# Sixteen gate tiles merged into eight pairs of seven block products, in a hybrid Hyena / attention layer on one Trainium2 core

## The chip, the core and the metric

The kernel runs on one core of one Trainium2 chip. TensorE (PE in the profile; its weight loads are PEld) multiplies a stationary 128x128 block, loaded from SBUF, with a moving operand of up to 512 columns and accumulates in PSUM, which has 8 banks of 512 fp32 columns for each of 128 partitions. VectorE (DVE), ScalarE (ACT) and GpSimd (POOL) work beside it, and SyncE (SP) issues most DMAs, in the order of its queue. [...] The metric is the device time of one execution in microseconds (us), less is better.

## The reference

One layer with two branches on the same modulated input, for a prompt of 128 tokens and a latent grid of 512 tokens (8 rows of 64), model width 1024, all in fp32:

```python
def layer_forward(x, cond, ctx_kv, p):
    shift, scale, gate = modulation(cond, p["w_ada"], p["b_ada"])     # silu(cond) @ w_ada + b_ada, in three parts
    h = x * (1 + scale) + shift
    (v_h, x1, x0, g_h), (q, k, v, g_a), m = split_projection(h, p["w_in"], p["conv_w"], p["conv_b"])
    h_fwd, h_bwd = hyena_filters(x.shape[1], ...)
    y_h = hyena_long_conv(v_h, x1, x0, h_fwd, h_bwd, p["hyena_d"])
    y_a = ...      # prompt: softmax attention; latent: window of 8 x 16 with a bias, and all cached context keys
    out = merge_branches(y_h, g_h, y_a.reshape(g_a.shape), g_a, m, p["w_bh"], p["w_ba"], p["w_out"])
    x_new = layer_norm(ALPHA * x + gate * out, p["ln_g"], p["ln_b"])

def merge_branches(y_h, g_h, y_a, g_a, m, w_bh, w_ba, w_out):
    p_h = (y_h * jax.nn.silu(g_h)) @ w_bh
    p_a = (y_a * jax.nn.silu(g_a)) @ w_ba
    m_h, m_a = jnp.split(jax.nn.sigmoid(m), 2, axis=-1)
    return (m_h * p_h + m_a * p_a) @ w_out
```

`split_projection` is one product of h (640 tokens x 1024) with `w_in` (1024 x 10240). Its last 2048 columns are m, the logits of the sigmoid gates m_h and m_a: they are what the change concerns most. `gate`, the third part of the modulation, scales the output of the layer, with one row for the prompt and one for the latent tokens. There are 16 heads of 64.

## The kernel before

**Numbers.** Values are held in fp32. A product is made of three passes in the type fp32r: each operand is split into a high part (ScalarE copy, L98) and a low part (VectorE subtraction, L99), and high x high, high x low and low x high are accumulated. `split` (L97) does it for a weight tile (128x1024: 8 blocks of 128x128 in input depth, k), once per tile.

**Projections.** `proj` (L171) computes 128 output channels for all 640 tokens: `wraw` loads the raw weight tile (512 KB) through SP's queue into a ring of two buffers, `wtile` splits it into rings of two (`wh`) and three (`wl`), and `accumulate` (L161) runs 8 k x 3 passes x 2 halves of 320 tokens, 48 matmuls 128x320 (L166), into the two banks of a double tile of the pool `ps_mm`, of which there are two. Four single banks (`ps_ax`, `aux`) serve attention and the rest. The tiles are numbered in `wall`: T_Q, T_K, T_V, T_GA (attention gates), T_MH and T_MA (the logits of m_h and m_a, 8 tiles each), T_BH and T_BA (the two branch projections), T_WO (the output).

**Stages.** A prologue makes the modulation and h (tiles `hH`, `hL`). Then come four quarters of the Hyena branch, whose results are the 8 rows-of-channels `yh`, kept in SBUF. Attention runs over eight pairs of heads, `attend(j)`, j = 0 to 7; each is cut into steps (`tiled`: scores, softmax on VectorE, ScalarE and GpSimd, and the values of earlier blocks; `turned`: transposes of the probabilities), and `weave` puts main work between the steps: the query, key, value and gate tiles of later heads for j < 7 (`mains`), and for j = 7 the eight T_MH tiles (`mix_h`). The results `ya` (`gated`, L868) stay in SBUF too. After attention come two T_MA tiles (`mix_a`), the eight T_BH tiles (with the merge by m_h at L993, and beside each a step of `gate_rows`), the rest of T_MA alternating with the T_BA tiles (L1022 to L1025), and the output tiles (`out_tile`, 48 matmuls of 512 columns for 128 tokens) with their norms (`norm_tile`).

**The output gate.** `gate_rows` (L970) loads the third part of `w_ada` in eight pieces of 512 KB and multiplies each by the conditioning `st` with 8 fp32 matmuls (`ada`, L231), which the trace holds as 16 records; `gate_bias` (L1002) then spreads the row of each group over 128 partitions with 12 matmuls and adds the bias, into `gbc`.

**What sets the order.** The Tile framework schedules all engines from a model of their times. TensorE's order is the program's own in the prologue and in attention (`manual_schedule`); elsewhere the scheduler orders it too. Loads are pinned to program order on SP while `pinned[0]` is true: until the filters, and not after.

## Time and profile before

| | us |
|---|---|
| median of 3 runs (least to most) | 925.89 (925.84 to 927.05) |
| the profiled execution, of which the span | 925.7, 923.9 |
| prologue, Hyena quarters (to about 390) | 390 |
| attention with its main work (390 to about 670) | 280 |
| rest of T_MH, first T_MA, first T_BH (670 to 704) | 34 |
| T_BH tiles (704 to 759) | 55 |
| T_MA and T_BA tiles, gate bias (759 to 860) | 101 |
| output tiles (860 to 915), last norm and store (to 924) | 64 |

Rows of the profile read like this. A chain row `751.34 7.23 PE mm L166 x48` is a start, a length, and what ran: 48 matmuls of line 166. A group row gives the line, engine, operation, `out<-in` by the program's names, the shape, the count, then the busy time and the mean ns of one, then the idle time ahead of it with what ended it. A wait row `PE pt L824 <- ACT ptsp L914: 0.4, 2, 0.2` is the total, the number and the longest of TensorE's waits for that releaser. A DMA row gives the KB of one and the median time from issue to landing.

### The profile page before, as it was taken

What the parts mean: (1) busy time and instruction counts of PE and PEld (TensorE: products, weight loads), DVE (VectorE), ACT (ScalarE), POOL (GpSimd) and SP (SyncE); (2) the same over time, 40 slices, a digit from 0 to 9 for tenths busy, and PEclk for the clock granted to TensorE, in tenths of its full rate; (3) what the DMA queues carried; (4) which work ended last, traced back from release to release, by engine and by line L of the source; (5) the groups of instructions that cost most, each with busy time, mean ns of one, the idle gap of its engine ahead of it and who ended that gap; (6) DMA issues with size and microseconds to landing.
All of it is one profiled execution on the core that took longest, in us unless ns stands there. A gap on an engine that the chain in (4) does not pass through costs nothing.

```text
span 923.9 us, 16758 instructions
## 1 busy us (share of the span) xinstructions
PE 910.2 (99%) x6856; PEld 877.4 (95%) x6856; DVE 486.4 (53%) x948; ACT 380.4 (41%) x776; POOL 146.2 (16%) x188
## 2 busy tenths in 40 slices
PE   8999999999999999999999999999999999999996
PEld 7899999999999999999999999999999999999885
DVE  4776775693796676445352533432261223335676
ACT  4485455554545334255454544444261112223200
POOL 0011010110010000474454543331000000000000
PEclk9999999999999999999999999999999999999998
DMA  8966664655465113242222221212123343224631
GB/s 320 380 161 135 128 149 98 137 133 123 100 141 126 50 49 85 86 122 67 71 68 69 67 70 58 72 49 70 48 69 113 120 146 99 72 69 116 205 114 69
DMA packets 36553, 102.13 MB, mean 111 GB/s; under 512 B 4316, under 2 KB 13020, under 8 KB 36477
## 3 DMA queue, kind: packets, MB, share of 16 engines
q1 hardware_dynamic: 32300, 86.35, 28.9%
q0 software_dynamic: 4032, 14.68, 9.8%
q8 instruction: 54, 0.88, 0.4%
q14 instruction: 23, 0.18, 0.1%
q10 hardware_dynamic: 144, 0.03, 0.0%
HBM read 97.38 MB, written 3.67 MB: 109 GB/s over the span
## 4 chain that ended last, share of the span: by engine, by line
PE 95%; DVE 2%; ACT 2%; issue 1%; POOL 0%; POOLq 0%
PE mm L166 65%; PE out L1065 6%; PE v L721 5%; PE s L788 2%; PE s L831 2%; PE pt L824 2%; PE ve L732 1%; PE adaT L236 1%; PE adaT L253 1%; PE yb L151 1%; PE yb L153 1%; PE yb L152 1%; PE gate L236 0%; PE fl L384 0%; PE fl L385 0%
## 5 line engine op out<-in xcount | busy, mean ns | idle before, releaser
L166 PE MATMUL mm<-hH,wh 128*128 128x320 f32 x1120 | 263.3, 313 | 0.9 <-ACT hH L312 0.6
L166 PE MATMUL mm<-hH,wl 128*128 128x320 f32 x1120 | 259.7, 310 | 0.4 <-DVE wl L99 0.4
L166 PE MATMUL mm<-hL,wh 128*128 128x320 f32 x1120 | 259.1, 310 | 0.0
L99 DVE TENSOR_TENSOR wl<-raw,wh 128x1024 fp32r<-128x1024 f32 x66 | 81.6, 1237 | 231.9 <-ACT wh L98 231.7
L166 PEld LDWEIGHTS mm<-hH,wh 128*128 128x128 f32 x1120 | 186.7, 188 | 6.2 <-issue 4.2
L166 PEld LDWEIGHTS mm<-hH,wl 128*128 128x128 f32 x1120 | 188.0, 188 | 1.4 <-DVE wl L99 1.1
L166 PEld LDWEIGHTS mm<-hL,wh 128*128 128x128 f32 x1120 | 188.2, 188 | 1.1 <-DVE hL L313 0.5
L98 ACT ACTIVATE wh<-raw 128x1024 fp32r<-128x1024 f32 x66 | 69.8, 1059 | 216.8 <-PE mm L166 95.9
L143 POOL DMA_DIRECT2D wl<-wall x28 | 24.3, 869 | 264.0 <-ACT wl L142 208.8
L144 ACT ACTIVATE wh<-raw 128x1024 fp32r<-128x1024 f32 x28 | 29.7, 1060 | 42.9 <-PE mm L166 42.7
L808 POOL TENSOR_SCALAR p<-p,sm 128x384 f32<-128x384 f32 x32 | 42.1, 1326 | 27.7 <-DVE sm L807 27.7
L1095 POOL TENSOR_TENSOR r<-r,bc 128x64 f32<-128x64 f32 x1 | 0.3, 320 | 249.7 <-ACT r L1094 249.7
L808 POOL TENSOR_SCALAR edge<-edge,sm 128x320 f32<-128x320 f32 x32 | 35.5, 1121 | 0.0
L474 DVE SCALAR_TENSOR_TENSOR x<-zs,pack,x 128x641 f32<-128x641 f32 x32 | 28.3, 884 | 12.1 <-ACT x L472 12.0
L826 ACT ACTIVATE pts<-pt 128x384 f32<-128x384 f32 x64 | 26.2, 502 | 11.0 <-PE pt L824 11.0
L142 ACT ACTIVATE wl<-raw 128x1024 fp32r<-128x1024 f32 x28 | 30.0, 1071 | 0.0
L166 PE MATMUL mm<-yhH,wh 128*128 128x320 f32 x128 | 29.9, 315 | 0.0
L166 PE MATMUL mm<-yaH,wh 128*128 128x320 f32 x128 | 29.2, 309 | 0.0
L166 PE MATMUL mm<-yhL,wh 128*128 128x320 f32 x128 | 29.2, 309 | 0.0
L166 PE MATMUL mm<-yaH,wl 128*128 128x320 f32 x128 | 29.2, 309 | 0.0
L166 PE MATMUL mm<-yaL,wh 128*128 128x320 f32 x128 | 29.2, 309 | 0.0
L166 PE MATMUL mm<-yhH,wl 128*128 128x320 f32 x128 | 29.2, 309 | 0.0
(330 smaller groups left out, 1677.7 us busy)
## 6 DMA issues: line engine op xcount, KB each, us to landing
raw<-wall SPq DMA_DIRECT2D x96, 512.0 KB, 3.6
wl<-wall POOLq DMA_DIRECT2D x28, 512.0 KB, 5.8
ada<-wada SPq DMA_DIRECT2D x16, 512.0 KB, 8.1
gate<-wada SPq DMA_DIRECT2D x8, 512.0 KB, 3.7
wo<-wall SPq DMA_DIRECT2D x8, 512.0 KB, 3.7
xt<-xT SPq DMA_DIRECT2D x8, 320.0 KB, 8.1
dec<-decay SPq DMA_DIRECT2D x20, 128.0 KB, 3.5
x<-xB SPq DMA_DIRECT2D x5, 512.0 KB, 3.8
```

What stands on the lines that cost most here:

```text
L98: hi = nc.scalar.activation(dst_h, src, AF.Copy)
L99: return hi, (eng or nc.vector).tensor_tensor(dst_l, src, f(dst_h), op=ALU.subtract)
L142: nc.scalar.activation(wl, raw[:], AF.Copy, scale=-1.0)
L143: nc.gpsimd.dma_start(wl, a["wall"][i], accum_op=ALU.add)
L144: nc.scalar.activation(wh, raw[:], AF.Copy)
L166: nc.tensor.matmul(ps[hf][:, :HALF], wt[k], x[:, hf * HALF : (hf + 1) * HALF], start=(i == 0 and k == 0), stop=(i == lead[2] and k == NK - ...
L474: nc.vector.scalar_tensor_tensor(d, zs[:, c : c + NG], convw[:, i, c : c + 1], d, op0=ALU.mult, op1=ALU.add)
L721: nc.tensor.matmul(ps[:, t // 2, t % 2 * 256 : t % 2 * 256 + 256], x[:, k, P * t : P * t + P], wk, start=first and t % 2 == 0, stop=last, ...
L788: nc.tensor.matmul(dst[h], x[rows(h), qs], y[rows(h), ks], start=i == 0, stop=i == 2, skip_group_check=True)
L808: nc.gpsimd.tensor_scalar_mul(pv, pv, sm[:, 2:3])
L826: nc.scalar.activation(ptS[:], pt[:, :384], AF.Copy)
L1065: ins = nc.tensor.matmul(dst, m[k][:, c0 : c0 + P], w[:, c : c + n], start=(first and k == 0), stop=(last and k == NK - 1), skip_group_che ...
```

## The change

The line numbers here are those of the changed kernel.

*Pairs.* `mix_h` and `mix_a` are gone. `pair_tile` computes two gate tiles (256 channels) at once. The weights (1024 x 256) and the tokens (1024 x 640) are seen as 2 x 2 blocks: two halves of the depth by two tiles, and two halves of the depth by two halves of the tokens. Seven products of blocks, each 4 k x 3 passes = 12 matmuls 128x320, stand in for eight; the price is sums: of weight blocks (`wsum`, VectorE), of token blocks (`token_sums`, once, beside attention heads 0 and 1), and of results (`u`, `c`). Each product accumulates in one bank. The tanh goes to `c` or `th`, which ScalarE's queue stores to DRAM (`mh_d`, `ma_d`), to be loaded again when the gates are merged.

*Places.* All eight pairs stand in attention: one ahead of the main work of each of j = 2 to 6, three in j = 7. `ps_mm` is four single banks.

*Room.* `yh` is stored to DRAM as it is made and loaded and split again late in attention and after it; `ya` is stored in blocks (`gated`, by SP, for j = 7 by ScalarE) and loaded in the T_BH loop.

*Output gate.* `gate_rows` no longer uses TensorE: at each T_BH tile it loads 128 rows of `w_ada` and does two multiply-adds on VectorE into `gbc`, a partial sum in each partition; the matmuls of `gate_bias`, 12 as before, add up the partitions.

*The end.* From the end of attention `pinned[0]` is true again, so all loads keep program order on SP. The output weights are loaded and split within the T_BA loop and behind it, and used in the order 0, 1, 2, 3, 4, 6, 7, 5.

```diff
-    ps_mm = ctx.enter_context(tc.tile_pool(name="ps_mm", bufs=2, space=PSUM))
+    ps_mm = ctx.enter_context(tc.tile_pool(name="ps_mm", bufs=4, space=PSUM))
...
+    def acc(name):
+        return ps_mm.tile([P, 512], F32, tag="mm", name=name)
...
     def gate_tile(i, dst, eng=None):
-        ps = (yield from proj(i, eng=eng))[2]
-        nc.scalar.activation(two(dst), ps[:, :, :HALF], AF.Tanh, scale=0.5)
-        nc.vector.scalar_tensor_tensor(two(dst), two(dst), 1.0, ps[:, :, :HALF], op0=ALU.add, op1=ALU.mult)
+        ps = yield from proj(i, eng=eng)
+        for p, cs in zip(ps, CS):
+            nc.scalar.activation(dst[:, cs], p[:, :HALF], AF.Tanh, scale=0.5)
+            gate(dst[:, cs], p)
...
             gapped_product(out["yh"][n], out[f"u{n // 2}"][n % 2])
+            nc.sync.dma_start(yh_d[n], out["yh"][n][:])
...
+    def gated(j, o_, *spans):
+        yo = tp.tile([P, P], F32, tag="yo", bufs=3, name=f"yo{j}")
...
+            nc.vector.tensor_tensor(yo[:, c0 : c0 + n], out[f"sg{j}"][:, cols], o_[:, c0 : c0 + n], op=ALU.mult)
+            (nc.scalar if j == 7 else nc.sync).dma_start(ya_d[j][:, cols], yo[:, c0 : c0 + n])
...
+    ORDER = ("b11", "t2", "t3", "t1", "b21", "t4", "b22")
+    RING = ("wh", "wl", "wl", "wh", "wl")
+
+    def pair_tile(i0, i1, use):
+        for i in (i0, i1):
+            if i not in raws:
+                wraw(i)
+        ra, rb = raws.pop(i0), raws.pop(i1)
...
+        wsum(2, a11, a21, ALU.subtract)
+        wsum(1, src[2], a22, ALU.subtract)
+        for j in range(3):
+            prep(j)
+        wsum(3, a21, a22, ALU.add)
+        wsum(6, a12, src[1], ALU.add, src[1])
+        for j in range(3, 5):
+            prep(j)
+        ps = {}
+        for j in range(7):
+            if j < 4:
+                ps["xyvz"[j]] = acc(f"sp{i0}_{j}")[:, :HALF]
+            dst, x = ps["xyvzxvz"[j]], operand(ORDER[j])
+            for k in range(4):
+                wh, wl = (wb[j][:, i, P * k : P * k + P] for i in range(2))
+                for i, (wk, xi) in enumerate(((wh, 0), (wh, 1), (wl, 0))):
+                    nc.tensor.matmul(
+                        dst, wk, x(xi, k), start=j < 4 and k == 0 and i == 0, stop=k == 3 and i == 2, skip_group_check=True,
+                    )
...
+            if j == 0:
+                u = halfrow("u", 1, "u")
+                nc.scalar.activation(u, dst, AF.Copy)
+            elif j == 1:
+                nc.vector.tensor_tensor(u, dst, u, op=ALU.add)
+            elif j == 4:
+                use(0, 0, dst)
+            else:
+                if j != 3:
+                    c = halfrow("c", 4, f"c{j}_")
+                nc.vector.tensor_tensor(c, dst, c if j == 3 else u, op=ALU.add)
+                if j != 2:
+                    use(*{3: (1, 1), 5: (1, 0), 6: (0, 1)}[j], c)
+            prep(j + 5)
...
+        def use(i, hf, src):
+            th = sp.tile([P, HALF], F32, tag="c", bufs=4, name=f"th{m}")[:] if hf == i == 0 else src
+            nc.scalar.activation(th, src, AF.Tanh, scale=0.5)
+            nc.scalar.dma_start(dst[n0 + i][:, CS[hf]], th)
...
-            7: ((mix_h(),), 7 * NK),
+            7: ((mix(5), mix(6), last_pair(mix(7))), 3 * N_PAIR),
...
+    pinned[0] = True
+    for n in range(4, 6):
+        yh_raw(n)
...
     def gate_rows():
-        for pair in range(2):
-            ps = aux(f"gate{pair}")
-            for i in range(4):
-                raw = wp.tile([P, D], F32, tag="raw", name=f"gate{pair}{i}")
-                ada(16 + 4 * pair + i, ps[:, i * P : i * P + P], raw[:])
-                yield
-            nc.scalar.activation(gpart[:, pair * 512 : pair * 512 + 512], ps[:], AF.Copy)
+        for k in range(NK):
+            raw = slot(0, "v", f"gate{k}")[:, :D]
+            load_to(raw, a["wgate"][k])
+            for c in range(2):
+                s_ = st[:, k, c : c + 1]
+                if k == 0:
+                    nc.vector.tensor_scalar_mul(gbc[:, c], raw, s_)
+                else:
+                    nc.vector.scalar_tensor_tensor(gbc[:, c], raw, s_, gbc[:, c], op0=ALU.mult, op1=ALU.add)
+            yield
...
     for n in range(NK):
-        th = out[f"mh{n}"]
-        ps = now(proj(T_BH + n, yhH, yhL))[2]
-        nc.vector.scalar_tensor_tensor(two(th), two(th), 1.0, ps[:, :, :HALF], op0=ALU.add, op1=ALU.mult)
+        ps = now(proj(T_BH + n, yhH, yhL))
+        wraw(T_BH + n + 2)
+        th = mixed(mh_d, n, "mh", NK)
+        mhs.append(th)
+        for p, cs in zip(ps, CS):
+            gate(th[:, cs], p)
+        raw = slot(1, ("q", "ql")[n % 2], f"yaraw{n}")
+        load_to(raw[:], ya_d[n])
+        split(yaH[n], yaL[n], raw[:])
         next(side, None)
...
+        if 0 < n < 5:
+            out_weight(n - 1)
         if n == 4:
             gate_bias()
...
+    for k in (4, 6, 7, 5):
+        out_weight(k)
```

## The prediction

> **What bounds the kernel now.** I read the page's busy shares and its clock row first, then the chain that ended last, then the waits of TensorE, and only then single stages.

> ```profile
> span 923.9 us, 16758 instructions
> PE 910.2 (99%) x6856; PEld 877.4 (95%) x6856; DVE 486.4 (53%) x948; ACT 380.4 (41%) x776; POOL 146.2 (16%) x188
> PEclk9999999999999999999999999999999999999998
> PE 95%; DVE 2%; ACT 2%; issue 1%; POOL 0%; POOLq 0%
> ```

> TensorE is busy 99% of the span at full granted clock, and 95% of the last chain is TensorE. The waits of TensorE, summed by what it waited for, say how much stall is left to gain. The first row is the largest of the span and lies in the prologue; the other two are the only ones of the attention:

> ```profile
> PE adaT L253 <- POOL spare L268: 1.5, 1, 1.5
> ...
> PE pt L824 <- ACT ptsp L914: 0.4, 2, 0.2
> ...
> PE mm L166 <- DVE sm L807: 0.2, 1, 0.2
> ```

> So the time is the number of matmuls times their pitch, plus a short end. The windows by stage (PE, weight loads, VectorE, ScalarE and GpSimd busy, then clock, DMA share, GB/s) show what room the other engines have where new work is put:

> ```profile
> 390.00:476.00 86.00, 85.82 (x691) 82.39 (x690) 37.23 (x130) 42.74 (x120) 48.68 (x54) 1.00 0.27 83
> 476.00:560.00 84.00, 84.00 (x735) 80.59 (x734) 35.00 (x131) 42.62 (x117) 39.38 (x45) 1.00 0.21 65
> 560.00:670.00 110.00, 109.57 (x893) 106.06 (x892) 33.54 (x101) 43.51 (x106) 24.81 (x25) 1.00 0.20 62
> 704.00:760.00 56.00, 56.00 (x470) 53.06 (x464) 15.32 (x16) 9.14 (x10) 0.00 (x0) 1.00 0.38 125
> 860.00:924.00 64.00, 55.60 (x264) 45.91 (x262) 42.81 (x77) 7.82 (x12) 0.93 (x2) 0.95 0.37 124
> ```

> Attention is 390 to about 670, the T_BH tiles 704 to 760, the output tiles 860 to 915. VectorE is under half busy in attention and a quarter busy in the T_BH stage. The pitch comes from the chain in order of time (start, length, what):

> ```profile
> 341.99 1.44 PE ve L732 x12
> ...
> 386.98 1.44 PE v L721 x12
> ...
> 642.15 1.31 PE pt L824 x12
> ...
> 650.50 1.46 PE ov L831 x24
> ...
> 704.50 7.23 PE mm L166 x48
> 712.30 7.23 PE mm L166 x48
> ...
> 751.34 7.23 PE mm L166 x48
> 759.14 70.62 PE mm L166 x480
> ...
> 859.78 55.84 PE out L1065 x264
> ```

> **The change part by part.** *Seven products instead of eight.* Sixteen gate tiles of 48 matmuls (768) become eight pairs of 7 x 4 x 3 = 84 (672), of the same form, 128x320. Undisturbed, 480 take 70.62 us: 0.1471 us each. 96 fewer are worth -14.1. All pairs stand where TensorE is the bound, so the whole of it counts, if what feeds them is on time. [...]

> *Twelve matmuls in a row into one bank.* Before, two halves alternated between banks. The two rows x12 above are the nearest: `ve` accumulates twelve in one bank, `v` changes bank, both 1.44. Price 0.

> *What feeds a pair.* Prices by groups (form, count | busy, mean ns):

> ```profile
> L99 DVE TENSOR_TENSOR wl<-raw,wh 128x1024 fp32r<-128x1024 f32 x66 | 81.6, 1237 | 231.9 <-ACT wh L98 231.7
> L99 DVE TENSOR_TENSOR sl<-sd,sh 128x512 fp32r<-128x512 f32 x20 | 13.8, 688 | 4.1 <-PE mm L166 3.1 <-ACT sh L98 0.9
> L98 ACT ACTIVATE sh<-sd 128x512 fp32r<-128x512 f32 x20 | 12.8, 638 | 17.6 <-DVE sd L390 11.7 <-PE yb L152 5.9
> L1024 DVE TENSOR_TENSOR mta<-mta,mh 128x640 f32<-128x640 f32 x8 | 6.6, 821 | 0.0
> L681 DVE SCALAR_TENSOR_TENSOR ql<-mm,q 128x320 fp32r<-128x320 f32 x8 | 3.9, 481 | 0.0
> ```

> Per pair VectorE gets 4 block sums and 7 low parts at 0.69 and 5 additions out of PSUM at 0.48, 10.0, and loses two low parts at 1.24: +7.5. Beside attention heads 6 and 7, the stretch 560 to 670, go four pairs: 33.5 + 30 of some 110. In 476 to 560 it is two pairs, 35 + 15. In 390 to 476 it gets one pair and the two token sums, each 9 additions and 4 low parts of 128x640 at 0.82, together 29: 66 of 86, the fullest. ScalarE gets about 2.5 per pair plus 4 store issues. No engine becomes the bound on average. Before a pair's first product stand the raw loads (3.6, below), two block sums and one split (0.64 + 0.69): 6.3. The preceding main tile takes 7.1 on TensorE and has attention steps beside it, so some 1 to 6 us are left (its steps, pt and ov in the chain, take 1.3 to 1.5 each). I price new waits in attention at +0.5, about the 0.6 that attention shows now; the ends are 0 and +7 (8 pairs at 0.9, each late by the length of six matmuls).

> The four PSUM banks, the stores and reloads of yh, ya, mh and ma, and the halved tanh and gate instructions cost 0: a product's bank is used again three products later (36 x 0.147 = 5.3), and each reload is issued a tile (7.06) or more ahead against 3.6 for a larger one. Where yh is reloaded for the first T_BH tiles, the low halves k = 4 to 7 are split after the last pair; TensorE has 72 matmuls (10.6) until it needs them, since T_BH 0 and 1 are interleaved there. If that cover fell short, it would cost what is missing once. The new DMAs on SP's queue (48 small ya stores, waiting for VectorE) stand ahead of weight loads; one late store delays the next load by as much, which the same 1 to 6 us must take.

> *Gate rows.* The ada matmuls go:

> ```profile
> L236 PE MATMUL gate<-gate,st 128*32 128x128 f32 x128 | 5.2, 279 | 0.0
> ```

> From the chain, T_BH tiles start 7.80 us apart (712.30 to 751.34 are five steps), a tile undisturbed takes 48 x 0.1471 = 7.06: 8 x 0.74 = -5.9. In their place each T_BH tile loads a 512 KB row block into a single buffer and does two multiply-adds 128x1024 (1.24 each by the low-part row):

> ```profile
> raw<-wall SPq DMA_DIRECT2D x96, 512.0 KB, 3.6
> ...
> gate<-wada SPq DMA_DIRECT2D x8, 512.0 KB, 3.7
> ...
> x<-xB SPq DMA_DIRECT2D x5, 512.0 KB, 3.8
> ...
> y<-r SPq DMA_DIRECT2D x4, 512.0 KB, 2.6
> ...
> bc<-rows SPq DMA_DIRECT2D x2, 512.0 KB, 5.6
> ```

> The loop is issue 0.34 + load 3.7 + 2.48 = 6.5, under 7.06. VectorE's sum per tile is 2.48 + 1.24 (weights) + 0.82 (ya) + 2 x 0.48 (gates) = 5.5. Cost 0; the other end is +4, if the loop is 7.5 long because the multiply-adds stand behind the gates in VectorE's order (8 x 0.5).

> *Start of T_BH 2.* In the new order T_BH 0 ends only 6 matmuls before T_BH 1. The third weight set can be split only then (two buffers): ScalarE 1.06 against 0.88 of cover, +0.2 at least; its low part stands behind two half gates on VectorE: 1.06 + 0.96 + 1.24 - 0.88 - 0.59 (the four matmuls that need only the high part) = 1.8 at most. I take +1.0, the middle, since the gates may start during the ScalarE copy.

> *The end.* SP's loads keep program order now, so the residual x of tile t + 1 is issued behind the store of y of tile t. Before, it was ahead:

> ```profile
> 895.75 0.33 SPq L63 DMA_DIRECT2D x<-xB  x1
> 900.36 12.00 SPq L1104 DMA_DIRECT2D y<-r  x2
> ```

> The same stretch in the timeline with VectorE:

> ```profile
> 905.57 1.29 DVE L1082 SCALAR_TENSOR_TENSOR r<-x,r 128x512 f32<-128x512 f32 x2
> ...
> 911.90 0.69 DVE L1082 SCALAR_TENSOR_TENSOR r<-x,r 128x512 f32<-128x512 f32 x1
> 912.01 0.34 SPq L1104 DMA_DIRECT2D y<-r  x1
> ...
> 915.64 0.42 DVE L1081 TENSOR_TENSOR r<-gbc,out 128x256 f32<-128x256 f32 x1 [1.03 <-PE out L1065]
> 917.01 0.23 DVE L1085 BATCH_NORM_AGGREGATE mv<-st 128x2 f32<-128x18 f32 x1
> ```

> The stores of y (two in the row of 900.36, the later one apart at 912.01) end their issue at 900.7 and 912.35. For tiles 1 to 3 the load (3.8) lands before the residual is needed: y stores are 11.1 us apart, and after each 5.2 us pass until the next residual (900.36 to 905.57 for tile 3). For the last tile the load goes out at 912.35 and lands at 916.15; then x, 512 + 256 + 256 columns, and the statistics of them follow, 1.4 + 1.4, so the aggregate comes at 918.9 instead of 917.01: +1.9. Behind y's own 512 KB it can be later: two such transfers in a row took 5.6 (the bc row) against 3.8, +3.7. I take the middle, +2.8.

> **Sum.** 925.7 (the profiled execution's own time, of which 923.9 is the span; the median of the runs is 925.9) - 14.1 - 5.9 + 0.5 + 1.0 + 2.8 = 910.0.

> **The rivals.** *Slower: a pair's weights come late.* VectorE's order has the block sums, which wait for both raw tiles, ahead of the softmax reductions, and SP's raw loads stand behind ya stores that wait for VectorE. If the 6.3 us chain stands half open at each pair, 8 x 3.2 = +25, 935. It becomes slower than before from 15.7 / 8 = 2.0 us per pair. For it: 66 of 86 in the first stretch and one ring for both raws. Against it: TensorE waits 0.6 in 280 us of attention now, with the same two buffers. A smaller case of it, 0.5 to 1.5 us per pair, gives 914 to 922.

> *The gate-row loop bounds the T_BH stage*, +3.5 to 4: 914. For it: 6.5 of 7.06 leaves little. Against: 15.3 of 56 busy there before.

> *The end is hidden*, because x of the last tile arrives in time or VectorE is late anyway: 907.

> *One bank, or short gaps, slow the matmuls.* The pairs' products change bank every twelve and end in waits; if the granted clock fell in pairs, 672 matmuls would need 15.7 / 672 = 23 ns more, a clock of 0.86, to end at no change, 926. [...] The traces show 1.00 in every stretch above in which TensorE is full, with bank changes at every matmul, and 0.95 only where it stops at the end.

> **How the numbers follow.** Forecast 0.60 (own range 907 to 914: the sum with T_BH 2 and the end at their bounds, and waits of 0 to 3); gate loop 0.08; end hidden 0.08; pairs a little late 0.08; pairs late past the balance 0.14; slower matmuls 0.02. All lower bounds (0, 0.2, 1.9) give 907.8 and with the end quite hidden 905.9; all upper ones (7, 1.8, 3.7, 4) give 922.2. The range 905.5 to 921 leaves out the late pairs and the slow matmuls. A change under 0.2% (1.85 us) can't be told from none here. Faster: 0.60 + 0.08 + 0.08 + 0.08 = 0.84; same 0.02; slower 0.14.

> **What the profile after would show.** The matmul count falls by 96 of 128x320 and the gate rows of L236 are gone; starts of T_BH tiles are 7.06 apart instead of 7.80; a wait of about 1 us on ScalarE or VectorE stands before T_BH 2; in attention the waits of TensorE stay under 1 us and none names the block sums; the end shows VectorE waiting for the DMA of x, and the stretch from TensorE's last matmul to the end grows from 8.3 (923.9 less 859.78 + 55.84) to about 11. I would be wrong if TensorE's waits in attention name the pair's weight parts or a raw load, at more than 2 us per pair, if VectorE comes near full in attention, or if T_BH tiles start over 7.1 apart with the multiply-adds as the releaser.

## The result, and the profile after

The changed kernel takes 914.01 us (median of 4 runs, 911.77 to 914.06) against 925.87 before (925.36 to 927.05): a ratio of 0.9865, 95% interval 0.9849 to 0.988. That is 11.9 us saved, where 15.7 were forecast (910.0, range 905.5 to 921).

The page of the changed kernel, the lines that answer to those shown of before:

```profile
span 911.8 us, 16892 instructions
PE 889.9 (98%) x6632; PEld 859.9 (94%) x6632; DVE 585.7 (64%) x1137; ACT 408.9 (45%) x869; POOL 160.4 (18%) x188
PEclk9999999999999999999999999999999999999998
```

TensorE lost 20.3 us of work (910.2 to 889.9), close to the 20.0 that seven products (14.1) and the gate rows (5.9) were to give. VectorE got 99 us more, and TensorE waits that it did not have:

```profile
PE pt L836 <- POOL p L820: 2.8, 3, 1.6
PE pt L836 <- ACT ptsp L928: 1.6, 1, 1.6
...
PE mm L168 <- DVE mh L481: 1.4, 1, 1.4
...
PE mm L168 <- DVE wl L102: 1.0, 2, 0.6
```

To see where the time went I took three marks from TensorE's instructions by tile (first and last start): the first score of attention, the first output matmul, the last output matmul. Before:

```profile
L788 PE MATMUL s<-k,q x80: 302/334/446, 390.7 to 632.4; 64*128 64x320 f32 x32, 64*128 64x384 f32 x32, 64*128 64x128 f32 x16
L1065 PE MATMUL out<-woh,yhH x33: 277/390/398, 859.6 to 915.1; 128*128 128x512 f32 x27, 128*128 128x256 f32 x6
L1065 PE MATMUL out<-woh,yhL x33: 277/389/398, 860.5 to 915.3; 128*128 128x512 f32 x27, 128*128 128x256 f32 x6
```

After:

```profile
L798 PE MATMUL s<-k,q x80: 302/333/445, 389.6 to 693.4; 64*128 64x320 f32 x32, 64*128 64x384 f32 x32, 64*128 64x128 f32 x16
L1250 PE MATMUL out<-woh,yhs x176: 278/393/402, 844.6 to 900.1; 128*128 128x512 f32 x144, 128*128 128x256 f32 x32
```

| stretch | before | after | difference |
|---|---|---|---|
| start to first score | 390.7 | 389.6 | -1.1 |
| first score to first output matmul | 468.9 | 455.0 | -13.9 |
| output matmuls | 55.7 | 55.5 | -0.2 |
| last output matmul to the end | 8.6 | 11.7 | +3.1 |

The second stretch is the sum by the measured waits: -14.1 - 5.9 + 4.4 (attention, where 0.6 were before) - 0.6 + 2.0 (T_BH) = -14.2. The end has grown as forecast. The 1.1 before attention has the size of one wait of the kernel before, in its Hyena quarters (TensorE for VectorE's `sl`, 1.1), which none of the later traces has; why it is gone was not looked into.

The matmuls of a pair run at the old pitch, twelve in a row into one bank. In the timeline of TensorE (start, length, what), 24 of them, two products, stand from the first of these rows up to the last:

```profile
710.37 0.31 PE L1034 MATMUL sp<-hH,wb 128*128 128x320 f32 x1
...
713.88 1.04 PE L1034 MATMUL sp<-t,wb 128*128 128x320 f32 x6
```

(713.88 - 710.37) / 24 = 0.146 us.

### The profile page after: what moved, and what is told of

It is laid out like the page before. It is cut to its first block, busy times and chain, and to the rows that moved or that the text cites. A ratio compares the mean times of both kernels' runs of the same rounds, so it can differ in the third digit from the quotient of the medians.

```text
span 911.8 us, 16892 instructions
## 1 busy us (share of the span) xinstructions
PE 889.9 (98%) x6632; PEld 859.9 (94%) x6632; DVE 585.7 (64%) x1137; ACT 408.9 (45%) x869; POOL 160.4 (18%) x188
## 5 line engine op out<-in xcount | busy, mean ns | idle before, releaser
L168 PE MATMUL mm<-hH,wh 128*128 128x320 f32 x864 | 204.3, 312 | 1.8 <-ACT zs L471 1.0
L168 PE MATMUL mm<-hH,wl 128*128 128x320 f32 x864 | 202.0, 310 | 0.4 <-DVE wl L102 0.4
L168 PE MATMUL mm<-hL,wh 128*128 128x320 f32 x864 | 202.3, 310 | 0.0
L168 PEld LDWEIGHTS mm<-hH,wl 128*128 128x128 f32 x864 | 145.6, 188 | 1.2 <-DVE wl L102 0.9
L168 PEld LDWEIGHTS mm<-hL,wh 128*128 128x128 f32 x864 | 145.4, 188 | 1.1 <-DVE hL L315 0.5
L1034 PE MATMUL sp<-t,wb 128*128 128x320 f32 x384 | 60.2, 310 | 0.0
L1034 PEld LDWEIGHTS sp<-t,wb 128*128 128x128 f32 x384 | 56.9, 188 | 0.2 <-issue 0.2
L168 PE MATMUL mm<-yhs,wh 128*128 128x320 f32 x256 | 48.7, 309 | 1.4 <-DVE mh L481 1.4
L1034 PE MATMUL sp<-hH,wb 128*128 128x320 f32 x192 | 48.4, 315 | 0.0
L1250 PE MATMUL out<-woh,yhs 128*128 128x512 f32 (+1 forms) x176 | 45.6, 373 | 0.0
## 6 DMA issues: line engine op xcount, KB each, us to landing
raw<-wall SPq DMA_DIRECT2D x96, 512.0 KB, 3.7
wl<-wall POOLq DMA_DIRECT2D x28, 512.0 KB, 5.7
ada<-wada SPq DMA_DIRECT2D x16, 512.0 KB, 8.1
gate<-wgate SPq DMA_DIRECT2D x8, 512.0 KB, 3.6
wo<-wall SPq DMA_DIRECT2D x8, 512.0 KB, 3.6
```

Source lines behind the costliest of these rows:

```text
L168: nc.tensor.matmul(ps[hf][:, :HALF], wt[k], x[:, hf * HALF : (hf + 1) * HALF], start=(i == 0 and k == 0), stop=(i == lead[2] and k == NK - ...
L1034: nc.tensor.matmul(dst, wk, x(xi, k), start=j < 4 and k == 0 and i == 0, stop=k == 3 and i == 2, skip_group_check=True,)
L1250: ins = nc.tensor.matmul(dst, m[k][:, c0 : c0 + P], w[:, c : c + n], start=(first and k == 0), stop=(last and k == 5), skip_group_check=True,)
```

## The experiments

Each is one edit of the changed kernel; the times are medians.

| kernel | us (least to most) |
|---|---|
| changed | 914.01 (911.77 to 914.06) |
| residual loads ahead | 910.73 (909.75 to 911.23) |
| gate rows one tile later | 912.51 (911.71 to 915.51) |
| pair after the gate tile | 911.88 (911.66 to 914.62) |
| scaling on ScalarE | 914.82 (913.63 to 919.48) |
| token sums left out | 910.77 (910.53 to 913.26) |
| token sums later | 911.80 (910.35 to 912.50) |
| eight products | 924.00 (922.63 to 925.17) |
| gate rows on TensorE | 916.48 (914.04 to 920.73) |
| four edits | 910.83 (909.70 to 911.18) |
| three edits | 910.25 (909.91 to 913.16) |
| three edits, token sums later | 908.01 (906.13 to 908.46) |

Executions of one of these kernels lie 1.5 to 6.7 us apart, so a single step is read from its trace, and the medians are a check.

### Eight products in the same places

```diff
-        return pair_tile(t0 + n0, t0 + n0 + 1, use)
+        for n in (2 * (m % 4), 2 * (m % 4) + 1):
+            ps = yield from proj(t0 + n)
+            for hf in range(2):
...
+                nc.scalar.activation(th, ps[hf][:, :HALF], AF.Tanh, scale=0.5)
+                nc.scalar.dma_start(dst[n][:, CS[hf]], th)
+            yield
...
-                return (alongside(plain, token_sums(j), 8),), 3 * NK
+                return (plain,), 3 * NK
```

> The eight pairs become sixteen plain tiles of 48 matmuls in the same places, without token sums and weight sums; everything else is as changed. By the sum, seven products save 14.1 and cost the waits in attention, 4.4 less the 0.6 that were there before: the time is 914.0 + 14.1 - 3.8 = 924.3. If the waits come from the places and the single banks rather than from the sums, they stay, and it is 928. If a matmul in a pair is slower than in a plain tile, it is under 922.

Measured: 924.0, as expected. TensorE's work says what the 96 matmuls are worth:

```profile
PE 903.8 (98%) x6728; PEld 874.0 (95%) x6728; DVE 508.0 (55%) x999; ACT 385.2 (42%) x813; POOL 146.7 (16%) x188
```

903.8 against 889.9 is 13.9, near the 14.1 of the sum. The time differs by 10.0 only, so the sums cost about 4. The waits of TensorE for GpSimd are gone from this trace, and two for ScalarE's copy of transposed prompt probabilities (`ptsp`) are left, 0.47 in j = 3 and 1.47 in j = 6: these 1.9 us come from the places and not from the sums, where the expectation had 0.6.

### Residual loads ahead

```diff
     tail.close()
+    pinned[0] = False
```

> Only the pinning of loads ends before the output tiles, so the residual of the last tile is issued ahead of the store of tile 2 again. If the longer end of the changed kernel (11.4 us from TensorE's last matmul to the end against 8.3 before) is the late residual: VectorE no longer waits for the DMA of x, the end is 8.3 us again, the time 914.0 - 3.1 = 910.9. Rival, VectorE's order in the end is itself longer (statistics after all three residual additions): the end stays over 10, the time about 913.

Measured: 910.73. The end of the changed kernel, SP's rows and VectorE's (start, length, and in brackets the idle time and what ended it):

```profile
897.47 0.34 SPq L1289 DMA_DIRECT2D y<-r  x1
897.86 0.42 SPq L63 DMA_DIRECT2D x<-xB  x1
...
902.22 1.36 DVE L1267 SCALAR_TENSOR_TENSOR r<-x,r 128x512 f32<-128x512 f32 x3 [1.41 <-DMA x<-xB]
...
904.87 0.23 DVE L1270 BATCH_NORM_AGGREGATE mv<-st 128x2 f32<-128x18 f32 x1
```

and of this kernel:

```profile
880.78 0.33 SPq L63 DMA_DIRECT2D x<-xB  x1
...
897.06 0.69 DVE L1268 SCALAR_TENSOR_TENSOR r<-x,r 128x512 f32<-128x512 f32 x1
...
902.19 0.24 DVE L1271 BATCH_NORM_AGGREGATE mv<-st 128x2 f32<-128x18 f32 x1
```

In the changed kernel the load goes out at 897.86, behind the store, and its data is used at 902.22, 4.4 later; nothing of the last tile's statistics can begin before. Here the residual's first part is done before TensorE ends. From the last output matmul to the end it is 909.1 - 900.5 = 8.6 again. The late residual is the whole of the longer end; the rival falls.

### Gate rows one tile later

```diff
-        next(side, None)
+        if n:
+            next(side, None)
```

> The gate-row steps start one T_BH tile later, the last of them in the T_BA loop. If the stall before T_BH 2 (1.4 for the gate's multiply that frees its bank, 0.6 for its low weights) comes from the first two row multiplies, which stand on VectorE ahead of that gate: the wait of 1.4 goes, 0.2 to 0.6 may stay, the time is 914.0 - 1.4 to -1.9 = 912.1 to 912.6. Rival, the third weight set is late because T_BH 0 and 1 are interleaved, as the prediction had it: the stall stays at 0.6 to 2 with ScalarE's wh or VectorE's wl as releaser, the time over 913.3.

Measured: 912.51. In the changed kernel's timeline ScalarE, VectorE and TensorE stand like this before T_BH 2:

```profile
741.04 1.06 ACT L101 ACTIVATE wh<-raw 128x1024 fp32r<-128x1024 f32 x1 [0.62 <-PE mm L168]
741.30 1.41 DVE L1154 TENSOR_SCALAR gbc<-gate,st 128x1024 f32<-128x1024 f32 x2
742.63 0.88 DVE L481 SCALAR_TENSOR_TENSOR mh<-mh,mm 128x320 f32<-128x320 f32 x2
743.26 0.87 PE L168 MATMUL mm<-yhs,wh 128*128 128x320 f32 x4 [1.38 <-DVE mh L481]
...
744.70 0.56 PE L168 MATMUL mm<-yhs,wl 128*128 128x320 f32 x2 [0.57 <-DVE wl L102]
```

With the rows later:

```profile
739.61 0.88 DVE L481 SCALAR_TENSOR_TENSOR mh<-mh,mm 128x320 f32<-128x320 f32 x2
740.52 1.88 PE L168 MATMUL mm<-yhs,wh 128*128 128x320 f32 x8 [0.27 <-DVE mh L481]
...
742.84 0.56 PE L168 MATMUL mm<-yhs,wl 128*128 128x320 f32 x2 [0.43 <-DVE wl L102]
```

T_BH 2 starts as soon as T_BH 0's bank has been read by the gate (L481), and in the changed kernel the first two row multiplies stand ahead of that gate. The wait falls from 1.38 to 0.27; 0.43 for the low weights stays. TensorE had stopped at 741.88 (743.26 - 1.38), and the high weights were split at 742.10 (741.04 + 1.06): 0.2 of the 1.38 would have been there for them alone, and the rest is a wait for the PSUM bank.

### Gate rows on TensorE again

```diff
-            for c in range(2):
-                s_ = st[:, k, c : c + 1]
...
+                ada(16 + 4 * pair + i, ps[:, i * P : i * P + P], raw)
```

> The output gate's rows go back to TensorE (64 small matmuls beside the T_BH tiles, their weights loaded into the changed kernel's own buffer), all else as changed. By the sum +5.9, less the 1.4 to 2.0 stall before T_BH 2 that the row multiplies cause: 914.0 + 5.9 - 1.7 = 918.2. If the rows on VectorE had cost time elsewhere in the T_BH stage or T_BA stage, it is less than 917; if that stall has another cause, 920.

Measured: 916.48, 1.7 under what was expected, and by its number the case "the rows on VectorE had cost time elsewhere". The trace of the stage speaks against that (first starts of T_BH and of T_BA matmuls):

```profile
L168 PE MATMUL mm<-yhs,wh x256: 304/309/416, 725.6 to 787.4; 128*128 128x320 f32 x128
L168 PE MATMUL mm<-ya_hH,wh x128: 305/309/416, 788.5 to 846.1; 128*128 128x320 f32 x128
```

62.9 for the eight tiles against 58.9 in the changed kernel (727.6 to 786.5): +4.0, near 5.9 less the 2.0 of waits. Most of the rest is in attention, where the edit changes nothing: this execution shows 2.8 us of waits there, and the changed kernel's 4.4.

### Token sums left out

```diff
-        tc.keep_in_program_order(nc.vector.tensor_tensor(t1, part(hH, 0, 1), part(hL, 0, 1), op=ALU.add))
...
-        nc.vector.tensor_tensor(t2, t1, part(hH, 0, 0), op=ALU.subtract)
...
+        for name, i, j in (("t1", 0, 0), ("t3", 1, 1), ("t2", 0, 1), ("t4", 1, 0)):
...
+            keep(name, part(hH, i, j))
```

> The 18 additions of the token sums are left out (the products then use unsummed token blocks, so the result is not the reference's); the splits into high and low parts stay. Theory, GpSimd's instructions are slowed while VectorE runs its two-operand additions: two multiplies of 128x320 in heads 0 and 1 take 2.1 to 2.5 again instead of 3.9, the waits for GpSimd fall from 2.8 to under 0.8, the time is about 911.7. Rival, GpSimd is late because of the order of its own queue, the bias tiles of the next head ahead of the scaling: 3.9 stays, the time stays within 0.5 of 914.0.

Measured: 910.77. The first 30 us of attention by windows (PE, weight loads, VectorE, ScalarE, GpSimd busy, with instructions), before:

```profile
390.00:420.00 30.00, 30.00 (x240) 28.55 (x239) 14.35 (x47) 15.22 (x45) 19.20 (x22) 1.00 0.37 108
```

in the changed kernel:

```profile
390.00:420.00 30.00, 27.39 (x204) 25.78 (x204) 23.28 (x52) 16.23 (x45) 24.96 (x20) 1.00 0.33 98
```

and with the sums left out:

```profile
390.00:420.00 30.00, 30.00 (x238) 28.75 (x235) 15.09 (x54) 15.26 (x48) 19.43 (x23) 1.00 0.39 119
```

GpSimd has the same work in all three (a few instructions of the second come after this stretch); it is busy 25.0 beside the sums and 19.4 without. Its instructions grow: the first two scalings of heads 0 and 1 in the changed kernel took, beside VectorE's additions,

```profile
399.61 0.82 DVE L956 TENSOR_TENSOR ts<-ts,hH 128x640 f32<-128x640 f32 x1
399.67 3.89 POOL L820 TENSOR_SCALAR edge<-edge,sm 128x320 f32<-128x320 f32 x2
...
405.80 0.55 PE L836 MATMUL pt<-pack,p 128*128 128x128 f32 x3 [1.63 <-POOL p L820]
```

3.89 us, and 2.13 in the kernel before:

```profile
399.79 2.13 POOL L808 TENSOR_SCALAR edge<-edge,sm 128x320 f32<-128x320 f32 x2
```

Two more such rows of the changed kernel, the first while VectorE was idle (from 413.49 to beyond 417), the second beside the next token sum's additions and splits on VectorE:

```profile
413.64 2.14 POOL L820 TENSOR_SCALAR edge<-edge,sm 128x320 f32<-128x320 f32 x2
...
426.61 4.02 POOL L820 TENSOR_SCALAR edge<-edge,sm 128x320 f32<-128x320 f32 x2
```

So beside VectorE's additions of two SBUF operands the scalings took 1.8 to 1.9 times as long on GpSimd (3.89 and 4.02 against 2.13 and 2.14). By what means they are slowed was not shown.

That the sums cause waits in this stretch is shown: TensorE loses nothing there in the four traces that don't have them there (without them, with eight products, and the two with later sums). How much they cost is not fixed. With the gate rows one tile later, an edit that changes nothing in attention, TensorE is busy 28.99 of the 30 us, and not 27.39:

```profile
390.00:420.00 30.00, 28.99 (x227) 27.22 (x226) 26.26 (x60) 15.94 (x45) 22.47 (x20) 1.00 0.36 104
```

GpSimd's order is the same, but its scaling of the prompt's probabilities ran beside other VectorE work, 2.80 in the changed kernel and 1.19 here:

```profile
396.32 2.80 POOL L871 TENSOR_SCALAR pp<-pp,smp 128x128 f32<-128x128 f32 x2
...
394.88 1.19 POOL L871 TENSOR_SCALAR pp<-pp,smp 128x128 f32<-128x128 f32 x2
```

TensorE then waited 0.28 for VectorE and 0.72 for ScalarE's `ptsp` at this place, and not for GpSimd. Over the traces with the sums in place the loss in this stretch is 1.0 to 2.6.

### Scaling on ScalarE

```diff
-            nc.gpsimd.tensor_scalar_mul(pv, pv, sm[:, 2:3])
+            if j < 2:
+                nc.scalar.activation(pv, pv, AF.Copy, scale=sm[:, 2:3])
+            else:
+                nc.gpsimd.tensor_scalar_mul(pv, pv, sm[:, 2:3])
```

> In heads 0 to 3 (the first two pairs) the scaling of the probabilities by the reciprocal of their sum is done by ScalarE instead of GpSimd. If TensorE's waits of 2.8 for that scaling are GpSimd's alone: they go, the time is 914.0 - 2.6 = 911.4. Rival, the chain reductions, exponential, reciprocal is late as a whole because VectorE and ScalarE are full: the transposes then wait as long for ScalarE, the time stays at 913.5 to 914.5.

Measured: 914.82, no gain, as the rival had it. GpSimd's part is out of the chain, and TensorE waits at the same place for something else:

```profile
403.23 0.21 DVE L819 RECIPROCAL sm<-sm 128x1 f32<-128x1 f32 x2
...
403.34 0.74 ACT L101 ACTIVATE t<-ts 128x640 fp32r<-128x640 f32 x1 [0.45 <-DVE ts L959]
403.98 1.10 ACT L821 ACTIVATE p<-p,sm 128x384 f32<-128x384 f32 x2
...
406.08 0.36 ACT L931 ACTIVATE ptsp<-ptp 128x256 f32<-128x256 f32 x1
...
406.50 0.55 PE L839 MATMUL pt<-pack,p 128*128 128x128 f32 x3 [1.58 <-ACT ptsp L931]
```

The reciprocals are done at 403.44, but the scaling stands on ScalarE behind the split of a token sum, which had waited 0.45 for VectorE's addition; behind the scaling and two exponentials stands the copy `ptsp`. So the sums delay the softmax in two ways, by the order on VectorE and ScalarE and by slowing GpSimd (3.89 us for 2.13, above); taking GpSimd out of it is not enough. The edit also gives ScalarE more to do (19.6 us busy in the first 30 of attention, 16.2 in the changed kernel), so a part of the new wait may be its own. How the 2.6 us divide was not separated.

### Token sums later

```diff
-            if j < 2 and h == 0:
+            if 0 < j < 3 and h == 0:
...
-            if j < 2:
-                return (alongside(plain, token_sums(j), 8),), 3 * NK
-            return (mix(0), plain), 3 * NK + N_PAIR
+            if j:
+                return (alongside(plain, token_sums(j - 1), 8),), 3 * NK
+            return (plain,), 3 * NK
...
-            3: ((mix(1), values(2), queries(5)), NK + N_VALUES + N_PAIR),
+            3: ((mix(0), mix(1), values(2), queries(5)), NK + N_VALUES + 2 * N_PAIR),
```

> The token sums stand beside heads 2 to 5 (j = 1 and 2) instead of 0 to 3, and the first pair moves from j = 2 to j = 3. In j = 0 GpSimd and VectorE have the most to do already (bias tiles, first reductions). If TensorE's waits in the first 30 us of attention come from the sums being in that stretch, they go there and at most 1 us comes back in j = 1 and 2: 912. If the sums cost the same wherever they stand, 914.0.

Measured: 911.80. The waits of the first 60 us of attention are gone; one of 1.7 comes back in j = 2, for a gate (`sg`, L481) that holds a bank:

```profile
465.59 0.63 ACT L101 ACTIVATE wb<-s 128x512 fp32r<-128x512 f32 x1 [2.03 <-DVE s L1007]
...
468.50 0.82 PE L168 MATMUL mm<-hH,wh 128*128 128x320 f32 x2 [1.72 <-DVE sg L481]
```

The gate's tanh stands on ScalarE behind this split, which waited 2.03 for a block sum of the next pair; on VectorE that block sum stood behind the last of the token sums, and the gate behind softmax reductions and a split. It is more than the 1 us expected.

### Pair after the gate tile

```diff
-            4: ((mix(2), gate_a(4), keys(5), queries(6)), 3 * NK + N_PAIR),
+            4: ((gate_a(4), mix(2), keys(5), queries(6)), 3 * NK + N_PAIR),
```

> In heads 8 and 9 (j = 4) the pair comes after the gate tile instead of first, so that its two raw weight tiles have one main tile more to arrive. TensorE's one wait there (1.6, for ScalarE's copy of transposed prompt probabilities) comes, by my theory, from that copy standing on ScalarE behind splits of the pair, which wait for VectorE's sums, which wait for the second raw load: it goes, the time is 912.4. Rival, the copy is late because ScalarE empties the values' banks just there: the wait stays, 914.0.

Measured: 911.88. The wait lies in the steps of j = 3 (heads 6 and 7), where the weights of the pair of j = 4 are prepared. In the changed kernel the second raw tile is late, VectorE's block sum waits for it, ScalarE's split waits for the sum, and the copy `ptsp` stands behind three splits and one short copy of values:

```profile
523.78 0.69 DVE L1007 TENSOR_TENSOR s<-raw,raw 128x512 f32<-128x512 f32 x1 [3.77 <-DMA raw<-wall]
...
525.23 0.63 ACT L101 ACTIVATE wb<-s 128x512 fp32r<-128x512 f32 x1 [0.98 <-DVE s L1007]
...
526.55 0.62 ACT L101 ACTIVATE wb<-s 128x512 fp32r<-128x512 f32 x1
527.07 0.37 ACT L928 ACTIVATE ptsp<-ptp 128x256 f32<-128x256 f32 x1
...
527.59 0.52 PE L836 MATMUL pt<-pack,p 128*128 128x128 f32 x3 [1.57 <-ACT ptsp L928]
```

With one main tile more the wait falls to 0.46.

### The edits together

The four edits (residual, gate rows, pair, scaling), then the first three, then these with the token sums later.

> The four edits together: residual loads ahead, gate rows one tile later, pair after the gate tile in j = 4, scaling by ScalarE for j = 0 and 1. If the four waits are independent and each is as its single run expects, -3.1 - 1.7 - 1.6 - 2.6 = -9.0: 905.0. If a removed wait only uncovers another that stood beside it, 907 to 910.

> Three of the four edits: residual loads ahead, gate rows one tile later, pair after the gate tile in j = 4; the scaling of probabilities stays on GpSimd. As the three waits lie in stages apart, their single gains should add: 914.0 - 3.1 - 1.4 - 1.3 = 908.2. If one of them only gives way to another wait, 909 to 911.

> fix3 and the later sums together: 908.2 - 2.0 = 906.2 if the sums are cheaper in j = 1 and 2; 908.2 if not.

Measured: 910.83, 910.25 and 908.01. They are 5.8, 2.0 and 1.8 us above what was expected if all gains add. For the four edits that sum had 2.6 for the scaling, which alone gained nothing; their trace has 3.5 of waits for `ptsp` in attention, as the scaling alone had 4.5. In the trace of the three edits each gain is there (1.1 ahead of T_BH, 1.3 in T_BH, 3.0 at the end, against the changed kernel), and 1.4 is lost again between the first T_BA and the first output matmul, where the matmuls of the gate bias stand; the cause was not looked for. The last one is the best version, 0.9794 of the kernel before (interval 0.978 to 0.9808). Its trace still has 1.7 of wait for the gate in j = 2, and half the clock after it (last section). By its median it fits the case that the sums are no cheaper (908.2), but it is 2.2 faster than the three edits, and two of its five executions took 906.1 and 906.4.

## Why the prediction came out as it did

*Right.* The pair's worth of -14.1 and the single bank's price of 0 (0.146 us a matmul, and 13.9 more of TensorE's work with eight products). The gate rows' -5.9, near the 5.5 of TensorE's work that came back with them (895.4 against 889.9). T_BH tiles are not bound by the loop of rows: without the 2.0 of waits they start 7.11 apart ((58.9 - 2.0) / 8). The end: +2.8 forecast, +3.1 measured, for the reason given, between its bounds of 1.9 and 3.7. The time lies in the range, but at the edge of the forecast's own 907 to 914.

*The same number by another way.* Another sum of the prediction also came to 914, with the gate-row loop as the bound, and the runs speak against it (the starts above).

*Mis-sized: waits in attention.* The step took +0.5 for new waits and left 0 to 7; the trace has 4.4, or 3.8 more than before, and the sign "under 1 us" failed. The step had VectorE's work as a total against the length of a stretch (66 of 86 in the fullest) and concluded that no engine becomes the bound. That is true and does not answer the question: the softmax of a block is a chain across VectorE, ScalarE and GpSimd, and each sum ahead of a reduction makes the chain later. The same windows row showed GpSimd busy 48.7 of 86, the fullest engine there beside TensorE, and the prediction gave it no line. The smaller case of the rival "a pair's weights come late" happened once, ahead of the pair of j = 4 (1.6), by way of the softmax; the greater part (2.8) came with the token sums, which no rival named (left out, the waits for GpSimd fell to 0.8, and in the first 30 us TensorE lost 1.0 to 2.6 in the traces with the sums there, and nothing in those without).

*Mis-sized and with the wrong cause: start of T_BH 2.* +1.0 forecast, 2.0 measured. The step had the third weight set late, by ScalarE's split at least 0.2; that 0.2 was there, but what ended the wait was the PSUM bank, held until the gate behind the row multiplies had read it (1.38). The low weights were late as it said (0.57).

*Missed: 1.1 less before attention.* No step had it, and without this luck the time would have been about 915.

Together: +3.3 for attention (3.8 less the 0.5 taken), +1.0 for T_BH 2, +0.3 at the end and -1.1 ahead of attention are 3.5 of the 4 us between 910.0 and 914.0; the rest is not assigned.

## What to carry to other kernels

Fewer matmuls are worth their pitch where TensorE is the bound, as here (13.9 us of its work for 96, at a pitch of 0.146); but the additions that replace them go to engines whose order other chains depend on, so look for the chain that runs through all of them (softmax) and not for the sum of busy time. Here a load stood behind a store in SP's order: the last tile's residual went out at 897.86, right after the store of y (897.47 to 897.81), and without the pinning at 880.78. So before pinning a queue's order, look for what the last load waits behind. Here a PSUM bank came free only when its last reader was done: a gate on a busy VectorE held TensorE for 1.38 us before T_BH 2 and, with the sums later, for 1.7 in j = 2. So look at what stands ahead of that reader on its engine.

## What the runs showed of the hardware

In three of the traces a stall cost more than its length. In the trace of the kernel with residual loads ahead, TensorE is busy for 1.72 of the 3.41 us around its stall before T_BH 2, and then the granted clock is 0.50 for 3.41 us, although TensorE is full (windows: PE, weight loads, VectorE, ScalarE, GpSimd, then clock):

```profile
740.65:744.06 3.41, 1.72 (x10) 1.19 (x9) 3.41 (x7) 2.40 (x3) 0.00 (x0) 1.00 0.60 195
744.06:747.47 3.41, 3.41 (x15) 3.41 (x14) 3.41 (x5) 0.00 (x0) 0.00 (x0) 0.50 0.73 233
```

The loss is half of 3.41, about 1.7 us: 15 matmuls, where 23 fit at the pitch of 0.147. In the changed kernel's own trace the same stall has no such consequence:

```profile
740.66:744.07 3.41, 2.04 (x13) 1.55 (x11) 3.38 (x6) 2.12 (x2) 0.00 (x0) 1.00 0.80 261
744.07:747.48 3.41, 2.84 (x20) 2.79 (x20) 3.41 (x6) 0.74 (x1) 0.00 (x0) 1.00 0.72 204
```

Two more of the traces show the dip, each right after a stall of 1.5 to 2 us (the pair after the gate tile, at T_BH 2, and the best version, at the gate in j = 2). By windows of 1 us the clock is 0.97, 0.50, 0.50, 0.50 and 0.82 from 742 to 747 in the one and 0.54, 0.50, 0.50 and 0.75 from 469 to 473 in the other, which is half for 3.4 us again. The others don't: their clock is 1.00 in every window of 10 us up to 900. In the 3.41 us ahead of the three dips TensorE was busy for 1.72, 1.55 and 1.72.

```profile
402.74:406.15 3.41, 1.78 (x15) 1.44 (x13) 3.41 (x9) 2.76 (x8) 3.41 (x3) 1.00 0.24 56
406.15:409.56 3.41, 2.43 (x18) 2.23 (x17) 2.57 (x6) 1.72 (x3) 3.41 (x4) 1.00 0.34 124
```

The edge of the two steps cuts the stall: in 3.41 us across it TensorE is busy for only 0.80.

```profile
404.10:407.51 3.41, 0.80 (x6) 0.50 (x6) 3.38 (x8) 1.89 (x6) 3.41 (x3) 1.00 0.49 153
```

In the kernel before, the step ahead of the fall has 0.92 and every other at least 2.29. So in these five traces the clock fell after 1.72 us or less, and in the two of them that were cut in steps it never fell after 1.78 or more, although the stretch across the edge is far less busy. What decides it outside these traces was not shown.

In each of the three kernels the execution with the dip is the slowest of those measured (914.62 with the pair after the gate tile, where the other three took 911.66 to 912.08). Whether those others had a dip too is not known (mean clock 0.992 to 0.995, against 0.993), so what the dip has to do with the spread between executions of one kernel was not shown.
